# Output projection between the last rounds of a recurrence, and attention at the recurrence's priority, in a four-layer trunk

## The chip, the cores and the metric

One core of one Trainium2 chip runs the kernel. The metric is device time of one execution in microseconds, the median of several runs. The engines are TensorE (PE, with its weight loads as PEld), VectorE (DVE), ScalarE (ACT), GpSimd (POOL) and SyncE (SP), which here issues the DMA transfers. Each engine takes its own instructions in order.

## What is computed

A diffusion trunk of four layers over 256 latent and 256 context tokens (512 columns in all) with 1024 channels. Every layer is a pair of token mixers side by side, an output projection with a gated residual, and a SwiGLU channel mixer:

```
for l in range(DEPTH):                      # 4
    h_ = modulate(rmsnorm(h, norm_mix[l]), shift, scale)
    if l % 2 == 0:  y = concat(rwkv7_mixer(h_ @ ...), na_mixer(h_ @ ...))   # 512 + 512 channels
    else:           y = concat(gdn_mixer(h_ @ ...), s5_mixer(h_ @ ...))
    h = h + gate * (y @ w_out[l])
    h = h + gate2 * swiglu(modulate(rmsnorm(h, norm_ffn[l]), shift2, scale2))
```

`shift`, `scale` and `gate` come from an adaLN product with the conditioning vector (`mod_w`, 25 MB per layer). The RWKV-7 mixer is a recurrence over the tokens in both directions with 8 heads of 64 channels:

```
sa = einsum('bhvk,bhk->bhv', s, a_t)
s = s * w_t[:, :, None, :] + sa[..., None] * b_t[:, :, None, :] + v_t[..., None] * k_t[:, :, None, :]
y = einsum('bhvk,bhk->bhv', s, r_t)
```

It ends in a readout: group norm over each head, a bonus term and a gate. The attention is a softmax over a window of the grid for latent tokens and over the context, 8 heads of 64 channels. The change concerns layers 0 and 2, the even ones.

## The kernel before

**Layout.** Activations lie channel-major: the residual `hT` is [128 channels, 8 tiles, 512 tokens]. Large products split weights and activations into a high and a low part and take three matmuls per channel tile (`gemm`, lines 222 to 224: high by high, low by high, high by low), in groups of 256 output columns. Weights come by DMA from DRAM into `w` (line 187), a cast on ACT makes `wh` (line 190) and a subtraction on DVE makes `wl` (line 191). PSUM has eight banks by use: g, h, x and o one each, f and b two each; when `n.wide` is set, large products alternate between b, b and g, h, otherwise between g and h alone.

**Mixer of an even layer.** `even_layer` (line 1849) has eight units of the recurrence, four pairs of heads by two directions. `Pipe.run(i)` (line 1827), for i from 0 to 9, runs `front` of unit i, and by turns `mid` of unit i-1 and `rec` of unit i-2 (`together`, line 1812: one round is one turn of each). `rec` is the chain over the chunks of tokens: a state product on PE (line 784), an update of the state on DVE (line 793), copies on ACT (line 789) and a readout product (line 790). A pair's readout follows its second direction: DVE, ACT and POOL (lines 802 to 833) with two gate matmuls on PE (line 832). All of `Pipe.run` stands under `high_priority(PRIO)`. Attention (`Na.heads`, line 980) follows `run(3)` to `run(6)`, one pair of heads each, without priority: scores (line 1007), maximum, exponential and division (lines 1014 to 1018), transposes (line 1021) and the product with V (line 1033). `pump` (in `trunk`) puts adaLN products (line 165) between. The tile scheduler orders the instructions of each engine by priority, program order and a simulated time.

**Behind the mixer.** Each mixer's output tile goes to DRAM (`Mixed.put`, line 54), RWKV tiles 0 to 3 and attention tiles 4 to 7. When all is done, `split_y` (line 341) loads them back as `ev` and splits each into `nh` and `nl`, a cast on ACT (line 270) and a subtraction on DVE (line 271). `restore_h` loads the residual from DRAM, and `out_proj` runs 4 column groups x 8 channel tiles x 6 matmuls = 192 matmuls of 128x512, whose results `add_h` (line 335) adds to `hT` in halves. Then come the norm (square sums at line 284) and the channel mixer.

```
yh, yl, loaded = n.split_y(yt, tok)
...
n.wide = True
n.out_proj(l, yh, yl, tok)
```

In the stretches below, unit k of the recurrence begins with its first line 790 matmul.

Of the kernel before, what the change touches and what calls it, by code (L numbers as in the profile page):

```python
# [42 lines left out]
class Mixed:  # L43
    """Outputs of the mixers, channel-major, kept in DRAM by channel tile."""

    def __init__(self, n, ntok):
        self.n, self.ntok = n, ntok
        self.d = [n.dram.tile([128, NT], F32, name=f"yd{k}") for k in range(KT)]
# [4 lines left out]
    def put(self, k, y):  # L53
        self.n.nc.sync.dma_start(self.d[k][:, :self.ntok], y[:, :self.ntok])


class Net:
    def __init__(self, tc, a, ctx):
# [6 lines left out]
        # banks of PSUM by use: large products, parts of the mixers, adaLN, outputs of the mixers  # L65
# [13 lines left out]

    def load_consts(self, name, pool, tag=None, width=None):  # L80
# [22 lines left out]
    def restore_h(self, pool, tok):  # L103
        self.hT = pool.tile([128, KT, NT], F32, name="hT")
        for k in range(0, KT, 2):
            self.nc.sync.dma_start(self.hT[:, k:k + 2, tok], self.hd[:, k:k + 2, tok])

    def load_h(self, pool):
        nc = self.nc
        self.hT = pool.tile([128, KT, NT], F32, name="hT")  # L110
# [69 lines left out]
    def unit(self, src, kt, cols):  # L180
        """src [128, kt, cols] in DRAM -> high and low tiles."""
# [12 lines left out]
    def mm3(self, out, pairs, start=True, stop=True):  # L194
        """out += sum over (lhsH, lhsL, rhsH, rhsL) of lhs.T @ rhs."""
# [7 lines left out]
    def gemm(self, W, kt, c0, cols, xh, xl, tok, done, order=None):  # L203
        """Columns c0.. of W (given as [128, kt, n]), channel-major: done(column tile, psum) for each 128."""
        nc = self.nc
        nt = tok.stop - tok.start
        for u0 in range(c0, c0 + cols, 256):
# [7 lines left out]
            for i0 in range(0, kt, ku):  # L215
                kn, k0 = min(ku, kt - i0), ks[i0]
                wh, wl = self.unit(W[:, k0:k0 + kn, u0:u0 + n], kn, n)
                for kk in range(kn):
                    i, k = i0 + kk, k0 + kk
                    for (m, mm), p in zip(ms, ps):  # L220
# [3 lines left out]
                        nc.tensor.matmul(o, wl[:, kk, m:m + mm], xh[:, k, tok], start=False, stop=i == kt - 1)  # L224
            for (m, mm), p in zip(ms, ps):
                done((u0 - c0 + m) // 128, p[:mm, :nt])

    def gemm_tok(self, W, c0, cols, xh, xl, done):
        """Columns of W, token-major: done(token tile, first column, width, psum)."""
# [21 lines left out]
    def vecs(self, pool, name, **src):  # L251
        """Vectors of multiples of 128 in DRAM, channel-major [128, n] each; they become attributes of the result."""
# [20 lines left out]
    def square_sums(self, tok):  # L273
        """Sums of h^2 over the channels, token-major: [128, token tile]."""
# [13 lines left out]
    def rstd_bcast(self, tok, ss=None):  # L288
        """1 / sqrt(mean of h^2 + eps) on all partitions: [128, tokens]."""
# [16 lines left out]
    def norm_mod(self, l, g, which, tok, ss=None):  # L306
        """nH, nL: high and low parts of the modulated RMSNorm, channel-major."""
# [31 lines left out]
    ORDER = (4, 5, 6, 7, 0, 1, 2, 3)  # L339

    def split_y(self, y, tok):
        yh = self.gp.tile([128, KT, NT], F32R, name="nh")
        yl = self.gp.tile([128, KT, NT], F32R, name="nl")
        for k in self.ORDER:
# [3 lines left out]
        return yh, yl, last.ins  # L348

    def out_proj(self, l, yh, yl, tok):  # L350
        W = self.a["w_out"][l].rearrange("(j p) n -> p j n", p=128)
        self.gemm(W, KT, 0, D, yh, yl, tok, lambda k, p: self.add_h(l, 16, k, p, tok), self.ORDER)
# [79 lines left out]
def rows(x):  # L432
    """The four rows of the grid in a padded line of tokens."""
# [3 lines left out]
def rwkv_consts():  # L437
# [4 lines left out]
    # for a and for r, by the chunk of a tile: the mask of b on the chunk's half of the partitions, that of k on the other  # L442
# [14 lines left out]
class Rwkv:  # L457
    """Both directions of the time mixing for one layer, by pairs of heads."""
# [3 lines left out]
    def __init__(self, net, e, pool):  # L462
        self.n, self.nc, self.p, self.e = net, net.nc, pool, e
        self.a = net.a
# [15 lines left out]
        self.shb = pool.tile([128, 3, PADDED], F32, name="shb")  # L480
# [10 lines left out]
    def project(self, key, i, col, nh, nl):  # L491
        """Column tile col of the input projection as tile i of a group."""
# [13 lines left out]
    def shifted(self, key, cols):  # L506
        """A group of projections, mixed with the shift of the tokens."""
        nc, n, sh, pd = self.nc, len(cols), self.shb, self.pd[key]
        rk = self.p.tile([128, 2, NT], F32, name="rk", bufs=2)
        p = [rk[:, 0], rk[:, 1]]  # L510
        if n == 3:
            p.append(self.p.tile([128, NT], F32, name="v"))
# [9 lines left out]
        for i, c in enumerate(cols):  # L522
# [7 lines left out]
            else:  # L530
                # the two chunks of each tile in each other's place
# [8 lines left out]
    def lora_in(self):  # L540
        nc = self.nc
        x = self.shifted("L", [12, 13])
        self.tw = self.p.tile([128, NT], F32, name="tw")
# [1508 lines left out]
```

## Time and profile before

| | |
|---|---|
| runs, us | 3426.96, 3420.39, 3414.71; median 3420.39 |
| profiled execution: span, first to last instruction | 3398.9 us, 21.5 below that median |
| profiled execution's own time | only its span is given |
| PE, DVE, ACT, POOL busy | 92%, 56%, 38%, 15% of the span |
| mean granted TensorE clock | 0.929 of full speed |
| DMA | 479 MB, 141 GB/s over the span |

A windows row gives a stretch, its length, then the busy time and number of instructions of each engine in it, the granted TensorE clock, the share of time that the DMA engines were busy, and GB/s. A row of groups gives line, engine, operation, output<-inputs, shapes and count, then total busy us, mean ns of one, and idle time before them with what ended it. A timeline row gives start, length, engine, line, operation; in brackets the idle time before it and what released it.

### The profile page before, as it was taken

To read this page: it belongs to the slowest core of one execution; us is meant where nothing else is said; L and a number is where in the kernel's file an instruction comes from. 1 tells how busy PE (TensorE), PEld (TensorE's weight loads), DVE (VectorE), ACT (ScalarE), POOL (GpSimd) and SP (SyncE) were. 2 spreads that over 40 slices of the span, in tenths; PEclk is the share of its full clock that TensorE was granted. 3 is DMA by queue.
4 is the path that set the end of the run, shared out by engine and by line. 5 is a ranking of instruction groups with operands and counts; after the bars stand their busy time and mean duration, and the time that the engine had idled before them with its cause. 6 is when DMAs were issued, how large, how long until landed. Compare 5 with 4: busy or idle time off the path is not lost. (4 is left out here: it accounts for less than half of the span.)

```text
span 3398.9 us, 63286 instructions
## 1 busy us (share of the span) xinstructions
PE 3120.2 (92%) x24452; PEld 2418.1 (71%) x24452; DVE 1920.1 (56%) x4229; ACT 1291.6 (38%) x2785; POOL 515.4 (15%) x1159
## 2 busy tenths in 40 slices
PE   7999789999999889899999998877999999977998
PEld 4876456787787667578887776545787777756997
DVE  3556545766436696343434556555676445685554
ACT  3334344332235335232223333434333224534444
POOL 0223310000001653000000123220000000563000
PEclk8998889999999899899998998889999999978999
DMA  8635655345345544733336634553334334644554
GB/s 282 178 97 130 151 141 156 87 136 143 111 125 143 167 126 144 245 119 94 96 100 191 184 103 128 126 125 101 102 127 136 111 113 145 196 156 156 160 176 134
DMA packets 549696, 479.21 MB, mean 141 GB/s; under 512 B 176533, under 2 KB 480531, under 8 KB 549395
## 3 DMA queue, kind: packets, MB, share of 16 engines
q1 hardware_dynamic: 549394, 475.17, 48.5%
q8 instruction: 193, 3.16, 0.4%
q14 instruction: 109, 0.89, 0.1%
HBM read 406.34 MB, written 72.90 MB: 141 GB/s over the span
## 5 line engine op out<-in xcount | busy, mean ns | idle before, releaser
L191 DVE TENSOR_TENSOR wl<-w,wh 128x512 fp32r<-128x512 f32 x786 | 545.8, 697 | 766.4 <-ACT wh L190 746.6
L190 ACT CAST wh<-w 128x512 fp32r<-128x512 f32 x786 | 484.5, 619 | 1159.7 <-PE pb L223 343.3
L222 PE MATMUL pg<-nh,wh 128*128 128x512 f32 (+2 forms) x760 | 294.6, 388 | 19.4 <-ACT nh L270 8.7
L222 PE MATMUL pb<-nh,wh 128*128 128x512 f32 (+1 forms) x832 | 305.3, 374 | 4.0 <-ACT nh L325 2.7
L223 PE MATMUL pb<-nl,wh 128*128 128x512 f32 (+1 forms) x832 | 306.5, 371 | 0.0
L224 PE MATMUL pb<-nh,wl 128*128 128x512 f32 (+1 forms) x832 | 299.8, 373 | 0.0
L223 PE MATMUL pg<-nl,wh 128*128 128x512 f32 (+2 forms) x760 | 291.4, 383 | 0.6 <-DVE gr L1179 0.6
L224 PE MATMUL pg<-nh,wl 128*128 128x512 f32 (+2 forms) x760 | 290.4, 382 | 0.1
L298 POOL TENSOR_TENSOR nr<-nv,cst_base 128x4 f32<-128x4 f32 (+1 forms) x9 | 8.4, 938 | 1660.8 <-DVE nv L296 1660.8
L222 PE MATMUL ph<-nh,wh 128*128 128x512 f32 (+1 forms) x624 | 242.0, 388 | 10.1 <-ACT nh L325 5.9
L224 PE MATMUL ph<-nh,wl 128*128 128x512 f32 (+1 forms) x624 | 240.1, 385 | 0.0
L223 PE MATMUL ph<-nl,wh 128*128 128x512 f32 (+1 forms) x624 | 239.5, 384 | 0.0
L165 PE MATMUL px<-mw,cnd 128*32 128x256 f32 x1536 | 158.8, 450 | 83.5 <-DMA mw<-in_mod_w_dram 68.9
L222 PEld LDWEIGHTS pg<-nh,wh 128*128 128x128 f32 (+1 forms) x760 | 146.3, 193 | 56.4 <-ACT nh L270 11.3
L222 PEld LDWEIGHTS pb<-nh,wh 128*128 128x128 f32 x832 | 158.6, 192 | 36.3 <-ACT nh L325 3.2
L223 PEld LDWEIGHTS pb<-nl,wh 128*128 128x128 f32 x832 | 159.5, 192 | 29.3 <-DVE nl L271 1.3
L224 PEld LDWEIGHTS pb<-nh,wl 128*128 128x128 f32 x832 | 155.5, 191 | 30.7 <-issue 1.0
L223 PEld LDWEIGHTS pg<-nl,wh 128*128 128x128 f32 (+1 forms) x760 | 146.1, 192 | 34.8 <-issue 3.0
L224 PEld LDWEIGHTS pg<-nh,wl 128*128 128x128 f32 (+1 forms) x760 | 145.7, 192 | 29.1 <-issue 1.0
L858 POOL TENSOR_TENSOR Etmp<-E 64x14 f32<-64x14 f32 (+13 forms) x448 | 160.6, 359 | 31.1
L860 POOL TENSOR_TENSOR E<-E,Etmp 64x14 f32<-64x14 f32 (+13 forms) x448 | 158.8, 354 | 32.9
L222 PEld LDWEIGHTS ph<-nh,wh 128*128 128x128 f32 x624 | 119.6, 192 | 39.7 <-ACT nh L325 6.7
(578 smaller groups left out, 6440.8 us busy)
## 6 DMA issues: line engine op xcount, KB each, us to landing
mw<-in_mod_w_dram SPq DMA_DIRECT2D x192, 512.0 KB
w<-in_f_gate_dram SPq DMA_DIRECT2D x176, 256.0 KB
w<-in_f_up_dram SPq DMA_DIRECT2D x176, 256.0 KB
w<-in_f_down_dram SPq DMA_DIRECT2D x176, 256.0 KB
w<-in_w_in_even_dram SPq DMA_DIRECT2D x104, 256.0 KB
w<-in_w_in_odd_dram SPq DMA_DIRECT2D x80, 256.0 KB
w<-in_w_out_dram SPq DMA_DIRECT2D x64, 256.0 KB
hd<-hT SPq DMA_DIRECT2D x32, 256.0 KB
```

The source lines that it names most:

```text
L165: nc.tensor.matmul(p[32 * c:32 * c + 32, :256], self.cnd[:, k, :], wt[:, 256 * c:256 * c + 256], start=k == 0, stop=k == KT - 1, skip_grou ...
L190: nc.scalar.copy(wh[:, :n], w[:, :n])
L191: nc.vector.tensor_tensor(wl[:, :n], w[:, :n], wh[:, :n].bitcast(F32), op=ALU.subtract)
L222: nc.tensor.matmul(o, wh[:, kk, m:m + mm], xh[:, k, tok], start=i == 0, stop=False)
L223: nc.tensor.matmul(o, wh[:, kk, m:m + mm], xl[:, k, tok], start=False, stop=False)
L224: nc.tensor.matmul(o, wl[:, kk, m:m + mm], xh[:, k, tok], start=False, stop=i == kt - 1)
L298: nc.gpsimd.tensor_tensor(r, v, self.mhalf[:, :nt], op=ALU.pow)
L858: nc.gpsimd.tensor_tensor(o, E[:, :s, s:s + 1].to_broadcast([m8, s, v]), E[:, s:s + 1, s + 1:].to_broadcast([m8, s, v]), op=ALU.mult)
L860: nc.gpsimd.tensor_tensor(E[:, :s, s + 1:], E[:, :s, s + 1:], o, op=ALU.add)
```

## The change

Three things move in the even layers.

- `out_proj` is made in two parts. `EARLY`, channel tiles 0, 1 and 4 to 7, is loaded, split and multiplied while `run(8)` and `run(9)` go on; `LATE`, tiles 2 and 3 of the last two pairs of heads, follows the mixer. `gemm` becomes a generator, `gemm_steps`, that yields after each channel tile (six matmuls); after each round of `together` the pipe takes two steps in `run(8)` and one in `run(9)`, at ordinary priority and behind the last PE instruction put so far. The early part has only banks g and h. Its sum is added to `hT`, and that of the late part again.
- The last two pairs' outputs are split straight into `nh` and `nl` (`Mixed.put` with `parts` set), with no way through DRAM.
- `na.heads` stands under `high_priority(PRIO)`, as the recurrence does.

So that room is there by then, `hT` has a pool of its own, and the recurrence's tiles that only `front` needs lie in a pool `evenf` that is closed after `run(7)`, as attention's pool is. In odd layers `out_first` with all tiles stands for `split_y` and `restore_h` as before.

```diff
     def put(self, k, y):
-        self.n.nc.sync.dma_start(self.d[k][:, :self.ntok], y[:, :self.ntok])
+        if self.parts:
+            yh, yl = (x[:, k, :self.ntok] for x in self.parts)
+            self.n.split(y[:, :self.ntok], yh, yl)
+        else:
+            self.n.nc.sync.dma_start(self.d[k][:, :self.ntok], y[:, :self.ntok])
...
+    def last_pe(self):
+
+        return next(i for i in reversed(self.nc.cur_bb.bb.instructions) if i.engine == mybir.EngineType.PE)
...
+                    if i < kt - 1:
+                        yield
             for (m, mm), p in zip(ms, ps):
                 done((u0 - c0 + m) // 128, p[:mm, :nt])
+            yield
...
-    def split_y(self, y, tok):
+    EARLY, LATE, ALL = (0, 1, 4, 5, 6, 7), (2, 3), (4, 5, 6, 7, 0, 1, 2, 3)
+
+    def out_first(self, l, y, tok, ks):
+
+        self.open_g(3)
+        self.open_h()
         yh = self.gp.tile([128, KT, NT], F32R, name="nh")
         yl = self.gp.tile([128, KT, NT], F32R, name="nl")
-        for k in self.ORDER:
+        for k in ks:
             t = self.gp.tile([128, PADDED], F32, name="ev", bufs=2)[:, :NT]
             last = self.nc.sync.dma_start(t[:, tok], y.d[k][:, tok])
             self.split(t[:, tok], yh[:, k, tok], yl[:, k, tok])
-        return yh, yl, last.ins
-
-    def out_proj(self, l, yh, yl, tok):
+        y.parts = yh, yl
+        with self.tc.issue_after(last.ins):
+            self.restore_h(tok)
+        return last.ins, self.out_proj(l, y, tok, ks)
...
+FILL = (2, 1)
...
         steps = [s for s in steps if next(s, steps) is not steps]
+        yield
...
-            together(*(getattr(self.m, f)(*u(i - k), self.S[u(i - k)[0]])
-                       for k, f in enumerate(self.m.parts, 1) if u(i - k)))
+            for r in together(*(getattr(self.m, f)(*u(i - k), self.S[u(i - k)[0]])
+                                for k, f in enumerate(self.m.parts, 1) if u(i - k))):
+                with self.n.tc.high_priority(-PRIO), self.n.tc.issue_after(self.n.last_pe()):
+                    for _ in range(FILL[i == len(self.units) + len(self.m.parts) - 1]):
+                        next(self.fill, None)
...
             for h in heads.get(i, ()):
-                na.heads(h, yt)
+                with n.tc.high_priority(PRIO):
+                    na.heads(h, yt)
             pump(3)
...
+            if i == 7:
+                first_.__exit__(None, None, None)
+                np_.__exit__(None, None, None)
+                loaded, pipe.fill = n.out_first(l, yt, tok, n.EARLY)
+        for _ in pipe.fill:
+            pass
+    return yt, loaded
...
             n.wide = True
-            n.out_proj(l, yh, yl, tok)
+            if l % 2:
+                loaded, proj = n.out_first(l, yt, tok, n.ALL)
+            else:
+                proj = n.out_proj(l, yt, tok, n.LATE)
+            for _ in proj:
+                pass
```

How many PE instructions of attention (lines 1007, 1021 and 1033) and of the output projection stand in each part of the program's order, before -> with the change:

| | unit 2 | unit 3 | unit 4 | unit 5 | unit 6 | unit 7 | last readout | behind it |
|---|---|---|---|---|---|---|---|---|
| layer 0, attention | 32 -> 45 | 38 -> 59 | 34 -> 47 | 34 -> 39 | 38 -> 16 | 16 -> 0 | 14 -> 0 | |
| layer 0, projection | | | | | 0 -> 24 | 0 -> 109 | 0 -> 17 | 192 -> 42 |
| layer 2, attention | 34 -> 64 | 34 -> 60 | 38 -> 50 | 32 -> 30 | 32 -> 0 | 16 -> 0 | 22 -> 0 | |
| layer 2, projection | | | | | 0 -> 94 | 0 -> 50 | 0 -> 6 | 192 -> 42 |

The order of PE in layer 2, inside the last unit's rounds, before (`st`, `Bst`, `Phi` are the state and its factors, `naP` the softmax, `naqk` queries and keys):

```order
L784 MATMUL pb<-Bst,Phi 64x64 x2
L1021 MATMUL pg<-cst_base,naP 128x128 x2
L784 MATMUL pb<-st,Phi 64x64 x2
L790 MATMUL po<-st_17575,RW 64x128
L784 MATMUL pb<-st,Phi 64x64 x2
L1007 MATMUL ph<-naqk,naqh 128x512
L1007 MATMUL ph<-naqk 128x512
L784 MATMUL pb<-st,Phi 64x64 x2
L790 MATMUL po<-st_17576,RW 64x128
L790 MATMUL po<-st_17573,RW 64x128
```

and with the change (lines 784, 790, 222 to 224 are now 815, 821, 237 to 239):

```order
L815 MATMUL pb<-Bst,Phi 64x64 x2
L237 MATMUL pg<-nh,wh 128x512
L238 MATMUL pg<-nl,wh 128x512
L239 MATMUL pg<-nh,wl 128x512
L237 MATMUL ph<-nh,wh 128x512
L238 MATMUL ph<-nl,wh 128x512
L239 MATMUL ph<-nh,wl 128x512
L815 MATMUL pb<-st,Phi 64x64 x2
L821 MATMUL po<-st_17612,RW 64x128
```

Scores and transposes of the attention are gone from the round, and one step of the projection, six matmuls, stands between two state products.

The order of DVE in layer 0, in the last unit's rounds, before:

```order
L793 SCALAR_TENSOR_TENSOR st<-pb,Dk,Bst 128x64
L1014 TENSOR_REDUCE mx<-pg 128x1
L793 SCALAR_TENSOR_TENSOR st<-pb,Dk,Bst 128x64 x2
L1017 RECIPROCAL sm<-sm 128x1
L1018 TENSOR_SCALAR naP<-naP,sm 128x512
L793 SCALAR_TENSOR_TENSOR st<-pb,Dk,Bst 128x64
L1014 TENSOR_REDUCE mx<-pg 128x1
```

and with the change (793 is now 824, 335 is 357, 191 is 206):

```order
L824 SCALAR_TENSOR_TENSOR st<-pb,Dk,Bst 128x64
L357 SCALAR_TENSOR_TENSOR hT<-ph,mod,hT 128x256 x2
L357 SCALAR_TENSOR_TENSOR hT<-pg,mod,hT 128x256 x2
L824 SCALAR_TENSOR_TENSOR st<-pb,Dk,Bst 128x64
L206 TENSOR_TENSOR wl<-w,wh 128x512 x2
L824 SCALAR_TENSOR_TENSOR st<-pb,Dk,Bst 128x64
L206 TENSOR_TENSOR wl<-w,wh 128x512
L357 SCALAR_TENSOR_TENSOR hT<-ph,mod,hT 128x256 x2
```

Between two state updates DVE had the softmax's maximum and division; it now has additions into the residual and subtractions that make the weights' low part.

## Rows read from the trace of the kernel before

**Rows 1.** The page: the span, and busy time of the engines.

```profile
span 3398.9 us, 63286 instructions
...
PE 3120.2 (92%) x24452; PEld 2418.1 (71%) x24452; DVE 1920.1 (56%) x4229; ACT 1291.6 (38%) x2785; POOL 515.4 (15%) x1159
```

**Rows 2.** Windows of layer 0: upstream, last rounds, tail, behind the mixer.

```profile
core 0: us, PE busy (x) PEld busy (x) DVE busy (x) ACT busy (x) POOL busy (x), PEclk, DMA share, GB/s
315.00:512.00 197.00, 159.07 (x2244) 101.58 (x2227) 111.70 (x289) 81.18 (x219) 53.62 (x130) 0.82 0.60 145
512.00:548.30 36.30, 34.59 (x437) 21.39 (x436) 20.30 (x56) 21.51 (x66) 0.00 (x0) 0.95 0.39 122
548.30:560.00 11.70, 7.00 (x38) 3.88 (x38) 8.21 (x16) 5.57 (x12) 2.07 (x1) 0.86 0.29 93
560.00:612.00 52.00, 51.39 (x237) 41.49 (x237) 23.87 (x68) 15.68 (x27) 0.00 (x0) 0.97 0.61 169
```

**Rows 3.** Windows of layer 2, the same four stretches, the same columns.

```profile
2108.60:2306.00 197.40, 160.26 (x2182) 102.67 (x2181) 113.27 (x287) 79.78 (x215) 52.65 (x128) 0.82 0.51 120
2306.00:2347.60 41.60, 32.78 (x401) 21.33 (x401) 20.70 (x58) 21.12 (x66) 4.60 (x4) 0.88 0.17 52
2347.60:2357.20 9.60, 7.13 (x45) 3.99 (x44) 6.02 (x14) 3.92 (x10) 2.07 (x1) 1.00 0.01 2
2357.20:2410.00 52.80, 46.32 (x210) 36.91 (x209) 25.71 (x71) 18.04 (x31) 0.00 (x0) 0.97 0.65 182
```

**Rows 4.** Timeline of PE, layer 2: last readout matmul, first of the output projection.

```profile
2356.62 0.59 PE L832 MATMUL pb<-sx,g 128*128 128x512 f32 x1
2362.27 0.76 PE L222 MATMUL pg<-nh,wh 128*128 128x512 f32 x1 [5.06 <-ACT nh L270]
```

**Rows 5.** Windows of PE, late stretches: lines 1007, 1021 and 1033, each both layers.

```profile
512.00:560.00 48.00, 5.18 (x16) 0.93 0.37 115
2306.00:2357.20 51.20, 5.78 (x18) 0.90 0.14 42
...
512.00:560.00 48.00, 5.37 (x28) 0.93 0.37 115
2306.00:2357.20 51.20, 5.39 (x28) 0.90 0.14 42
...
512.00:560.00 48.00, 8.31 (x48) 0.93 0.37 115
2306.00:2357.20 51.20, 8.48 (x48) 0.90 0.14 42
```

**Rows 6.** Timeline of PE, layer 0: output projection at its own pace.

```profile
573.03 0.39 PE L224 MATMUL ph<-nh,wl 128*128 128x512 f32 x1
...
581.43 0.39 PE L224 MATMUL ph<-nh,wl 128*128 128x512 f32 x1
```

**Rows 7.** Groups by line, DVE then ACT, over the whole span.

```profile
L335 DVE SCALAR_TENSOR_TENSOR hT<-pb,mod,hT 128x256 f32<-128x256 f32 x140 | 58.6, 477 | 33.3 <-PE pb L224 33.3
...
L1018 DVE TENSOR_SCALAR naP<-naP,sm 128x512 f32<-128x512 f32 (+1 forms) x64 | 27.1, 423 | 1.6
...
L271 DVE TENSOR_TENSOR nl<-ev,nh 128x512 fp32r<-128x512 f32 (+1 forms) x32 | 19.6, 625 | 32.8 <-ACT nh L270 32.5
...
L1014 DVE TENSOR_REDUCE mx<-pg 128x1 f32<-128x512 f32 (+1 forms) x32 | 17.7, 553 | 4.6 <-PE pg L1007 4.1
...
L1016 ACT ACTIVATE naP<-ph,mx 128x512 f32<-128x512 f32 (+1 forms) x32 | 18.6, 580 | 22.6 <-DVE mx L1014 22.0
...
L270 ACT CAST nh<-ev 128x512 fp32r<-128x512 f32 (+1 forms) x32 | 18.1, 567 | 41.9 <-DMA ev<-yd 41.6
```

**Rows 8.** Timeline of layer 2, unit 7: two state updates that follow each other.

```profile
2341.06 0.28 DVE L793 SCALAR_TENSOR_TENSOR st<-pb,Dk,Bst 128x64 f32<-128x64 f32 x1
...
2341.85 0.27 DVE L793 SCALAR_TENSOR_TENSOR st<-pb,Dk,Bst 128x64 f32<-128x64 f32 x1
```

**Rows 9.** Waits of PE, layer 0, upstream and last rounds: total, times, longest.

```profile
PE px L165 <- DMA mw<-in_mod_w_dram: 26.1, 15, 5.5
PE pg L1007 <- ACT naP L1016: 4.6, 3, 3.5
```

More of the change, by code (lines that the diff above doesn't have):

```diff
@@ L78, in close_g, with open_h, close_h @@
         self.gp = None
+    def open_h(self):
+        self.hc_ = self.tc.tile_pool(name="h", bufs=1, side="right")
+        self.hT = self.hc_.__enter__().tile([128, KT, NT], F32, name="hT")
+    def close_h(self):
+        self.hc_.__exit__(None, None, None)
+    def last_pe(self):
+        return next(i for i in reversed(self.nc.cur_bb.bb.instructions) if i.engine == mybir.EngineType.PE)
     def load_consts(self, name, pool, tag=None, width=None):
@@ L101, in save_h, with restore_h @@
         self.hd = hd
-    def restore_h(self, pool, tok):
-        self.hT = pool.tile([128, KT, NT], F32, name="hT")
+    def restore_h(self, tok):
         for k in range(0, KT, 2):
@@ L460, with __init__ @@
     parts = ("mid", "rec")
-    def __init__(self, net, e, pool):
+    def __init__(self, net, e, pool, first):
         self.n, self.nc, self.p, self.e = net, net.nc, pool, e
+        self.pf = first
         self.a = net.a
@@ L479, in __init__ @@
         self.W = a["w_in_even"][e].rearrange("(j p) n -> p j n", p=128)
-        self.shb = pool.tile([128, 3, PADDED], F32, name="shb")
+        self.shb = first.tile([128, 3, PADDED], F32, name="shb")
         self.sts = [pool.tile([128, 128], F32, name=f"st{i}") for i in range(4)]
@@ L542, in lora_in @@
         x = self.shifted("L", [12, 13])
-        self.tw = self.p.tile([128, NT], F32, name="tw")
+        self.tw = self.pf.tile([128, NT], F32, name="tw")
         nc.scalar.activation(self.tw[0:64], x[0][0:64], AF.Tanh)
@@ L582, in pre @@
         r, k, v = self.shifted(hp, [hp, 4 + hp, 8 + hp])
-        lora = pl.tile([128, 2, 128], F32, name="lora", bufs=2)
+        lora = self.pf.tile([128, 2, 128], F32, name="lora", bufs=2)
         g2 = pl.tile([128, 128], F32, name="g2", bufs=2)
@@ L610, in front @@
         nc, n, pl = self.nc, self.n, self.p
-        t1 = lambda name: pl.tile([128, NT], F32, name=name)
+        t1 = lambda name: self.pf.tile([128, NT], F32, name=name)
         ch = lambda x: x.rearrange("p (c t) -> p c t", t=64)
@@ L643, in front @@
         ar, X["r"] = self.ar[:, 0:k4 + 1:k4], self.ar[:, k4]
-        bk = pl.tile([128, 8, 2, 64], F32, name="bk")
+        bk = self.pf.tile([128, 8, 2, 64], F32, name="bk")
         bq = bk.rearrange("p (t c) b s -> p t (c b) s", c=2)
@@ L1825, in __init__ @@
         self.S, self.late = {}, None
+        self.fill = iter(())
     def run(self, i):
@@ L1997, in trunk @@
             n.save_h()
+            n.close_h()
             fp.__exit__(None, None, None)
-            yt = odd_layer(n, l, nh, nl, pump, weights) if l % 2 else even_layer(n, l, nh, nl, pump)
-            n.open_g(3)
-            yh, yl, loaded = n.split_y(yt, tok)
+            layer = odd_layer if l % 2 else even_layer
+            yt, loaded = layer(n, l, nh, nl, pump, tok, *((weights,) if l % 2 else ()))
             fp = tc.tile_pool(name=f"f{l + 1}", bufs=1)
             f = fp.__enter__()
-            with tc.issue_after(loaded):
-                n.restore_h(f, tok)
             n.wide = True
-            n.out_proj(l, yh, yl, tok)
+            if l % 2:
[3 more added lines that the diff above has]
+            for _ in proj:
+                pass
             pump(8)
@@ L2025, in trunk @@
         fp.__exit__(None, None, None)
+        n.close_h()
         n.close_g()
```

28 lines of the change are left out of this document (15 added, 13 removed).

## The prediction, made before the change was run

> **What bounds the kernel now.** I read the page first: TensorE (PE) is busy 3120.2 of 3398.9 us [rows 1], so only work that PE does not repeat, and PE's idle time, can move the end. Then I cut layers 0 and 2 into stretches by the recurrence's own instructions and read each engine's busy time in them [rows 2, 3]. Four stretches matter per layer: *upstream* (units 2 to 5 of the recurrence, whose rounds also carry the next units' front and mid), the *last rounds* (units 6 and 7), the *tail* (last readout, from the last state product to the last L832), and what follows the mixer. In layer 0 they last 197.00, 36.30, 11.70 and 52.00 us with PE busy 159.07, 34.59, 7.00 and 51.39; in layer 2 197.40, 41.60, 9.60 and 52.80 with 160.26, 32.78, 7.13 and 46.32. So PE has 37.9 and 37.1 us idle upstream, 1.7 and 8.8 us in the last rounds, 4.7 and 2.5 us in the tails. Behind the mixer PE is full but for one hole in layer 2: 5.06 us before its first output-projection matmul, which waits for a cast of a tile that has just been to DRAM and back [rows 4].
>
> The last rounds are not empty. They carry attention: 18.86 us of PE in the late stretches of layer 0 (5.18 + 5.37 + 8.31) and 19.65 us in layer 2 (5.78 + 5.39 + 8.48) [rows 5]. To put 150 projection matmuls there, the change must first send that attention upstream. The question is what it costs there.
>
> **The change, part by part.**
>
> *Projection leaves the end.* Of 192 matmuls per even layer, 150 stand ahead of the last L832 and 42 behind it. They take one every 0.2333 us (573.03 to 581.43 us holds 36) [rows 6], so 150 x 0.2333 = 35.0 us leave the stretch behind the mixer, in each layer. Tiles 2 and 3 are now split straight from the readout. Behind the last readout the projection waits for a cast and a subtraction (0.567 + 0.625 us) [rows 7] and a start, 1.5 us in all; the 5.06 us hole of layer 2 goes. Layer 0: -35.0 + 1.5 = -33.5. Layer 2: -35.0 + 1.5 - 5.06 = -38.5.
>
> *Last rounds.* Layer 0: 38 rows of attention leave them (54 of 68 late rows stood in rounds, 16 stay), at 18.86/68 = 0.277 us each 10.5 us; 133 projection matmuls enter, 31.0 us. PE 34.59 - 10.5 + 31.0 = 55.1 us. Layer 2: 48 rows at 19.65/70 = 0.281 leave, 13.5 us; 144 matmuls enter, 33.6 us: 32.78 - 13.5 + 33.6 = 52.9 us. Idle time that stays: at least 0, at most the 8.8 us of layer 2's own rounds; I take 2.5, near the 1.7 of layer 0's, whose PE also had other work in the queue at every step. The state's own steps come every 0.8 us with nothing between (2341.06 to 2341.85) [rows 8], below the 1.4 us of the six matmuls put between them, so PE and not the state chain sets these rounds. Layer 0: 57.6 for 36.30, **+21.3**. Layer 2: 55.4 for 41.60, **+13.8**.
>
> *Tails.* Attention leaves (14 and 22 rows), 17 and 6 projection matmuls enter: about PE's 7 us again or less, beside a chain of DVE, ACT and POOL that sets the length. 0.
>
> *Attention upstream.* 52 rows (14.4 us) in layer 0 and 70 (19.65 us) in layer 2 move into stretches with 37.9 and 37.1 us of idle PE. Lowest: 0, all of it falls into holes; a gain is excluded, since none of its work goes (a rise of the clock is a rival below). The longest wait there is for adaLN weights still in transfer, 26.1 us in 15 waits [rows 9], which other work can fill. Highest as PE work: all of it, 34.1 us. With equal priority the program's order decides, and attention then stands ahead of the next unit's chain, not behind it: not only holes are filled. I take half: +7.2 and +9.8.
>
> *Second accumulation.* Two passes over the channels mean 16 more additions into the residual per layer, 32 x 0.477 = 15.3 us of DVE [rows 7]. With subtractions and weight splits DVE stays near 35 of some 55 us in the last rounds, so 0; cover gone, this is a rival below. The casts, subtractions, 12 weight loads, 6 reloads of mixer tiles and 4 of the residual per layer are moved, not added (four stores and four reloads even go), and pass SP's queue earlier, in stretches whose DMA share is 0.39 and 0.17: 0. Two odd layers: the same instructions, 0.
>
> Layer 0: -33.5 + 21.3 + 7.2 = -5.0. Layer 2: -38.5 + 13.8 + 9.8 = -14.9. **Sum -19.9 us.** It is made against the profiled execution; its span is 21.5 us below the median of the runs (3420.4), and I let that distance stand: **3400 us**. Bounds of the terms: idle in the rounds 0 to 8.8 (-5 to +12.6 in both layers), attention 0 to all (-17 to +17).
>
> **The rivals.**
>
> *A: the clock rises in fuller rounds.* The granted clock is 0.82 upstream in both layers, 0.95 and 0.88 in the last rounds, 0.97 behind them [rows 2, 3]. Busy time above full clock is about 0.18 x 159.07 + 0.05 x 34.59 + 0.18 x 160.26 + 0.12 x 32.78 = 63 us. If denser rounds win half of it back, the time falls by a further 31.5 us: 3400 - 32 = 3368. For it: the densest stretches (51.39 of 52.00 busy) have the highest clock. Against it: layer 0's stretch at 0.82 is 81% busy, as layer 2's, and it is 128-wide transposes and small products that are added upstream. The Trainium skill ("TensorE: Matmul & The Clock Gate", Loop structure matters more than you think) holds that matmuls kept back to back stay at the high clock, which by itself would give this time; the rows agree for the projection, 0.97. The same page (Part 4: PE-mode transpose) says that transposes do not count as busy in the same way, which would leave the upstream clock where it is.
>
> *B: attention stands in the recurrence's way: slower.* Engines take instructions in order. What moves upstream (122 rows, 6.5 per query tile, 18.8 tiles) is 34.1 us of PE, 18.8 x (0.553 + 0.423) = 18.3 us of DVE and 18.8 x 0.580 = 10.9 us of ACT [rows 7], and a row of one engine waits for another: a scores product that waits for the softmax of the tile before (4.6 us in three waits already) [rows 9] now blocks the chain behind it. If all PE work and half of the 29.2 us of DVE and ACT come on the path, 48.7 us stand in place of my 17.0: 3400 + 32 = 3432. It turns the sign from 37 us upstream on, and 47 us would be measured as slower. For it: equal priority and program order. Against it: 75 us of idle PE and DVE at 57% upstream.
>
> *C: the projection stalls in the last rounds.* The early pass has two PSUM banks, g and h, where the wide pass behind the mixer alternates with two more; all four column groups must be drained by four additions of 0.477 us before the next may start: 1.9 us x 8 = 15.3 us. If the reloads are late as in layer 2 before, add 5.06 per layer: 25.4 us, 3425, no difference to be measured. For it: additions queue on an in-order DVE behind state updates. Against it: a blocked PE also has adaLN products and the state's products to do, if they stand ahead of the blocked row.
>
> That the change doesn't do what it says is excluded by the order: 150 of 192 matmuls do stand ahead of the last readout, in both layers.
>
> **How the numbers follow.** A difference under 0.3% (10 us) can't be told from none here: faster is below 3410, slower above 3431. Forecast 0.47, its own range 3386 to 3412 from the bounds above (both ends together are unlikely); A 0.16, B 0.19, C 0.18. Faster: the forecast's part below 3410 (0.43) and A, 0.59. B and C lie about the upper bound: of B 0.12 and of C 0.07 end above 3431, slower 0.19. Same is what is left, 0.04 + 0.07 + 0.11 = 0.22. To leave 2 in 10 out, the range reaches to A and to B: 3362 to 3434.
>
> **What would show it.** Right: in the changed profile some 42 projection matmuls behind the last L863 per layer, 10 to 12 us from there to the first square sums' work instead of some 45; last rounds of 55 to 60 us with PE idle under 4; upstream stretches of 204 and 207 us. A would show as an upstream clock above 0.86. B as upstream stretches above 215 us, with PE waiting for naP or for the state. C as PE waiting in the last rounds for L357's additions or for hT and ev. The forecast is wrong if the upstream stretches don't lengthen at all, or if the last rounds grow by more than the matmuls put into them.

## The result, and the profile of the changed kernel

The changed kernel takes 3457.8 us (median of 4 runs, 3455.0 to 3465.0) against 3423.6 for the kernel before: a ratio of **1.0102, interval 1.0078 to 1.0127**. It is slower by 1.0%, and outside the predicted range.

The page of the changed kernel, answering to [rows 1]:

```profile
span 3457.7 us, 63374 instructions
...
PE 3164.3 (92%) x24452; PEld 2440.6 (71%) x24452; DVE 1933.9 (56%) x4261; ACT 1289.6 (37%) x2785; POOL 516.2 (15%) x1159
```

The profile of before that the prediction was made from has a span of 3398.9 us, some 20 us under the runs that were timed. A second profile of the same kernel (the run `again` below) has 3412.7, and stretches are compared with that one. Windows of it, first the five stretches of layer 0, then of layer 2 (from the norm to unit 1, units 2 to 5, last rounds, tail, behind the mixer; columns as in [rows 2]):

```profile
22.30:314.50 292.20, 268.79 (x2607) 201.72 (x2607) 156.55 (x354) 108.46 (x240) 60.06 (x165) 0.93 0.60 167
314.50:514.10 199.60, 165.79 (x2214) 106.06 (x2206) 110.47 (x288) 81.24 (x219) 50.90 (x130) 0.79 0.60 143
514.10:550.50 36.40, 34.88 (x438) 21.50 (x436) 20.32 (x56) 21.54 (x66) 0.00 (x0) 0.94 0.39 119
550.50:562.20 11.70, 7.00 (x37) 3.92 (x38) 8.33 (x16) 5.56 (x12) 2.07 (x1) 0.88 0.27 88
562.20:620.80 58.60, 55.69 (x261) 44.48 (x260) 26.16 (x74) 17.50 (x30) 1.01 (x1) 0.97 0.57 160
...
1841.90:2114.60 272.70, 260.93 (x2472) 198.40 (x2471) 149.97 (x341) 106.52 (x235) 57.92 (x164) 0.93 0.57 155
2114.60:2310.30 195.70, 160.50 (x2181) 102.33 (x2179) 114.51 (x288) 79.83 (x215) 52.66 (x127) 0.81 0.52 121
2310.30:2352.70 42.40, 33.85 (x402) 21.88 (x402) 20.70 (x58) 21.17 (x66) 4.61 (x4) 0.84 0.17 52
2352.70:2362.30 9.60, 7.11 (x44) 3.96 (x44) 6.02 (x14) 3.89 (x10) 2.07 (x1) 1.00 0.01 2
2362.30:2426.60 64.30, 56.12 (x261) 44.93 (x261) 29.30 (x78) 20.36 (x36) 1.01 (x1) 0.95 0.57 162
```

The same ten stretches of the changed kernel:

```profile
22.90:333.00 310.10, 273.76 (x2622) 205.63 (x2620) 160.23 (x364) 107.45 (x240) 61.28 (x170) 0.90 0.56 156
333.00:538.20 205.20, 176.29 (x2239) 112.00 (x2237) 118.73 (x307) 91.98 (x247) 52.72 (x125) 0.83 0.57 140
538.20:599.30 61.10, 60.33 (x554) 41.65 (x550) 26.45 (x59) 24.36 (x64) 0.00 (x0) 1.00 0.56 187
599.30:611.60 12.30, 8.56 (x28) 5.54 (x29) 7.82 (x16) 2.25 (x4) 2.07 (x1) 0.79 0.21 64
611.60:634.00 22.40, 19.56 (x111) 16.68 (x110) 14.27 (x56) 7.94 (x13) 1.01 (x1) 0.88 0.43 76
...
1873.50:2155.80 282.30, 262.04 (x2542) 196.48 (x2541) 156.35 (x351) 107.47 (x238) 59.86 (x161) 0.94 0.55 147
2155.80:2380.30 224.50, 192.11 (x2279) 122.39 (x2278) 124.54 (x325) 95.24 (x254) 50.09 (x129) 0.76 0.52 126
2380.30:2435.90 55.60, 55.50 (x419) 39.58 (x419) 23.72 (x53) 20.12 (x53) 0.00 (x0) 0.96 0.32 101
2435.90:2447.20 11.30, 5.73 (x17) 3.52 (x18) 6.20 (x12) 1.45 (x3) 2.14 (x1) 0.80 0.09 23
2447.20:2469.00 21.80, 19.46 (x112) 16.45 (x110) 14.29 (x56) 7.95 (x14) 1.01 (x1) 0.89 0.45 78
```

Read as differences, what was meant to happen did: the end is shorter by 36.2 and 42.5 us, the last rounds longer by 24.7 and 13.2, with PE busy for all but 0.8 and 0.1 us of them. The losses stand elsewhere. Units 2 to 5, which took the attention, are longer by 5.6 and 28.8 us; from the norm to unit 1, where nothing was to change, 17.9 and 9.6 are lost. Layer 0 comes out 12.6 us longer, layer 2 10.8. And layer 1, whose code the change hardly touches, is 17.8 us longer, layer 3 1.8. That is 43.0 of the 45.0 us between the two spans. The medians of the timed runs are only 34.2 us apart, so some 11 us of these differences are scatter of single profiles. The DMA hole of layer 2 [rows 4] is gone; the timeline of PE in the changed kernel:

```profile
2445.14 2.08 PE L863 MATMUL pb<-sx,g 128*128 128x512 f32 x2
2446.22 1.42 PE L237 MATMUL pb<-nh,wh 128*128 128x512 f32 x1
2447.44 0.63 PE L238 MATMUL pb<-nl,wh 128*128 128x512 f32 x1
2447.86 0.63 PE L239 MATMUL pb<-nh,wl 128*128 128x512 f32 x1
2448.29 0.63 PE L237 MATMUL pb<-nh,wh 128*128 128x512 f32 x1
```

### The profile page after: what moved, and what is told of

Same layout as the page of the kernel before. It is cut to its first block, busy times and chain, and to the rows that moved or that the text cites. A ratio compares the mean times of both kernels' runs of the same rounds, so it can differ in the third digit from the quotient of the medians.

```text
span 3457.7 us, 63374 instructions
## 1 busy us (share of the span) xinstructions
PE 3164.3 (92%) x24452; PEld 2440.6 (71%) x24452; DVE 1933.9 (56%) x4261; ACT 1289.6 (37%) x2785; POOL 516.2 (15%) x1159
## 5 line engine op out<-in xcount | busy, mean ns | idle before, releaser
L237 PE MATMUL pg<-nh,wh 128*128 128x512 f32 (+1 forms) x784 | 306.7, 391 | 9.6 <-ACT nh L347 3.3
L239 PE MATMUL pg<-nh,wl 128*128 128x512 f32 (+1 forms) x784 | 301.4, 384 | 2.1 <-DVE wl L206 2.1
L238 PE MATMUL pg<-nl,wh 128*128 128x512 f32 (+1 forms) x784 | 301.7, 385 | 1.5 <-DVE nl L293 1.0
L237 PE MATMUL ph<-nh,wh 128*128 128x512 f32 (+2 forms) x648 | 253.6, 391 | 12.4 <-ACT nh L347 6.1
L238 PE MATMUL ph<-nl,wh 128*128 128x512 f32 (+2 forms) x648 | 251.2, 388 | 0.7 <-DVE nl L348 0.7
L239 PE MATMUL ph<-nh,wl 128*128 128x512 f32 (+2 forms) x648 | 251.2, 388 | 0.3 <-DVE wl L206 0.3
L237 PEld LDWEIGHTS pg<-nh,wh 128*128 128x128 f32 x784 | 151.8, 194 | 49.2 <-issue 6.9
L238 PEld LDWEIGHTS pg<-nl,wh 128*128 128x128 f32 x784 | 151.6, 193 | 36.2 <-issue 3.2
L239 PEld LDWEIGHTS pg<-nh,wl 128*128 128x128 f32 x784 | 151.3, 193 | 35.1 <-DVE wl L206 3.0
L237 PEld LDWEIGHTS pb<-nh,wh 128*128 128x128 f32 x784 | 149.2, 192 | 34.2 <-ACT nh L347 3.4
L237 PEld LDWEIGHTS ph<-nh,wh 128*128 128x128 f32 (+1 forms) x648 | 125.2, 193 | 44.1 <-ACT nh L347 7.3
```

What stands on the lines that cost most here:

```text
L237: nc.tensor.matmul(o, wh[:, kk, m:m + mm], xh[:, k, tok], start=i == 0, stop=False)
L238: nc.tensor.matmul(o, wh[:, kk, m:m + mm], xl[:, k, tok], start=False, stop=False)
```

## The experiments

Three theories were put to the test. *Theory 1*: attention at the recurrence's priority costs more upstream than the end gains (the prediction's rival B). *Theory 2*: the two passes of the projection cost. *Theory 3*: the scheduler, which orders every engine by a simulated time, deals a new order in all four layers as soon as anything is edited, and the loss is that of the new deal.

### The parts of the change

**The kernel before again** (no edit):

> The kernel before, unchanged, for a second profile: is its first one (span 3398.9 us, 21 to 25 below the median of its runs) a fair base for a comparison by stretches? If so the mixers of layers 1 and 3 (end of the norm's broadcast to the next one) again last 422.0 and 351.0 us, and units 1 to 5 of layers 0 and 2 together 508 us (254.7 and 253.3). If that profile was a lucky one, the 20 us lie somewhere here, and what looked like a loss in the odd layers (+20.6 and +9.9 us in the changed kernel) shrinks by as much.

3414.6 us, span 3412.7, layers 1 and 3 at 424.8 and 359.1 us. So the first profile was 8 us lucky in layer 3, and what looked like a loss of 9.9 us there is 1.8. The loss in layer 1 stays.

**Without the attention's priority**:

```diff
-                with n.tc.high_priority(PRIO):
-                    na.heads(h, yt)
+                na.heads(h, yt)
```

> The change without the attention's priority. The order leaves 82 and 70 attention matmuls in or behind unit 6, and only 24 and 26 projection matmuls get ahead of the last readout. Theory 1 (attention at the recurrence's priority is what costs, in units 1 to 5): units 1 to 5 return to the lengths of before within 8 us per layer, and the whole to 3415 to 3435 us. Theory 2 (the two passes of the projection, its two banks and its 32 more additions cost): still some 20 us above before, 3440 to 3455. Theory 3 (the odd layers, dealt anew, cost 30 us whatever is done to the even ones): layer 1, whose order is near that of before, is back at 422, layer 3, whose order is near that of the change, stays at 360; total 3435 to 3445.

3479.5 us, 1.0186 (1.0164 to 1.0207): the worst but one, above all three expectations. Windows of its two tails:

```profile
576.90:608.90 32.00, 21.40 (x79) 13.26 (x80) 16.27 (x34) 13.03 (x28) 2.15 (x1) 0.73 0.29 90
...
2404.00:2428.20 24.20, 16.13 (x72) 10.78 (x72) 12.87 (x25) 10.64 (x22) 2.15 (x1) 0.79 0.44 134
```

Attention is now still running when the early pass is issued, both end up in the tail of the chain, and the tails take 32.0 and 24.2 us instead of 11.7 and 9.6. As dealt here, the early pass needs the priority. With so few projection matmuls ahead, the run can't tell what the priority itself costs.

**The attention's priority alone** (that edit, in the kernel before):

> The kernel before with the attention's priority alone; the projection stays behind the mixer (42 matmuls of layer 2 slip ahead by themselves), and no attention is left from unit 6 (layer 0) or 7 (layer 2) on. Theory 1: units 1 to 5 are 20 to 35 us longer per layer than before, the last rounds shorter by the attention that has left them (10 to 14 us per layer); total 3450 to 3475 us. Theory 2: no second pass, so no loss: 3410 to 3430. Theory 3: the even layers within 5 us of before, the odd ones longer by 10 to 30.

3443.7 us, 1.0075 (1.0054 to 1.0097). Up to unit 5 layer 0 loses 24 us, layer 2 only 10; layer 2 as a whole is 11 us *faster* than before (573.7 for 584.6), with 42 matmuls of its projection ahead by themselves, and layer 1 is 16 us slower (441.1) with not a line of it changed. No theory had all of that. Theory 2 is not needed for a loss: there is no second pass here.

**The projection held behind the mixer**:

```diff
-FILL = (2, 1)
+FILL = (0, 0)
...
-        for _ in pipe.fill:
-            pass
+        with n.tc.issue_after(n.last_pe()):
+            for _ in pipe.fill:
+                pass
```

> The change with every matmul of the output projection held behind the mixer, so that attention goes upstream and nothing takes its place in the last rounds. Theory 1: units 1 to 5 as long as in the changed kernel (+24 and +36 us, less where its order differs), last rounds 24 to 30 us instead of 61 and 56, 192 matmuls (45 us) behind the mixer instead of 42; total above the changed kernel by 0 to 15 us, 3458 to 3475. Theory 2: two passes without interleaving; near 3430. Theory 3: its layer 1 has an order of its own (half like that of the change), so it need not be 442; a value near 422 would say that the loss there hangs on the deal.

3458.6 us, 1.0127 (1.0102 to 1.0151), at the lower end of what Theory 1 expected and far from Theory 2's 3430. Layer 1 is at 438.0. Its window of the last rounds of layer 0, now without attention and without projection:

```profile
530.60:568.50 37.90, 32.05 (x420) 20.05 (x416) 15.32 (x37) 17.83 (x53) 0.00 (x0) 0.83 0.71 236
```

They last 37.9 us, where they lasted 36.4 with attention in them: in that order the attention had cost nothing there. (In the five other orders of the kernel before, below, these rounds take 43.7 to 47.6 us.) In layer 2 they shrink, 42.4 to 34.6. From here to the changed kernel the early pass adds 23.2 and 21.0 us to the rounds for 133 and 144 matmuls (31 and 34 us of work) and takes 38 and 39 off the end: between a quarter and two fifths of the pass's work is hidden, as far as two kernels with an order each can say.

### An empty edit, and the change by layer

**An empty edit of the kernel before**:

```diff
-                na.heads(h, yt)
+                with n.tc.high_priority(0):
+                    na.heads(h, yt)
```

> The kernel before with an empty edit: attention stands under a priority of 0, the same instructions, the same priority, but the scheduler deals another order (12, 40, 28, 40, 34 and 20 attention matmuls in units 2 to 7 of layer 0 for 32, 38, 34, 34, 38 and 16, 32 in and behind the last readout for 14; half of a quarter of the order of layer 1 changes too). Theory 3, widened after the first four runs (each edit makes the scheduler deal anew, and most of the loss is the new deal, not the moved work): 3435 to 3470 us, layer 1's mixer near the 435 us that the run without the attention's priority showed with the same order, layer 0's above 605. Theory 1 (the attention's priority costs): no priority, no loss: 3411 to 3427 us and layers 0 and 1 within 5 us of before.

3454.4 us, **1.0105** (1.0065 to 1.0144). The computation is the same, and each engine has as many instructions of work as before; their order alone differs, and the loss is that of the whole change. (The edit is not quite empty for the scheduler: `high_priority` sets the running count of priorities back when it is left, so what follows the attention ranks level with it.) Layer 0 takes 616.9 us and layer 1 438.6, as Theory 3 expected. Its page:

```profile
span 3436.0 us, 63333 instructions
...
PE 3126.1 (91%) x24452; PEld 2409.8 (70%) x24452; DVE 1919.6 (56%) x4229; ACT 1293.3 (38%) x2785; POOL 518.2 (15%) x1159
```

Span less busy time is PE's idle time: 309.9 us, where the second profile of before has 276.7. So an order alone can lose as much as the whole change. What the moved work costs in the changed kernel is not yet shown by that.

**The priority in layer 2 alone**, in the kernel before:

```diff
-                na.heads(h, yt)
+                if l == 2:
+                    with n.tc.high_priority(PRIO):
+                        na.heads(h, yt)
+                else:
+                    na.heads(h, yt)
```

> The kernel before with the attention's priority in layer 2 alone; the order of layers 0 and 1 is that of before, instruction for instruction. Theory 3: layers 0 and 1 within 4 us of before (598 and 424); layer 2 as its deal falls, near the 574 us of the run with the priority in both layers, whose layer 2 has much the same placing: total 3405 to 3420. Theory 1: layer 2's units 1 to 5 are 15 to 35 us longer, total 3430 to 3455.

3421.2 us, 1.0016 (0.9992 to 1.0039): no difference, against Theory 1 and 1 us above Theory 3's range. Layer 2 takes 579.7 us, 5 under before, again with 42 projection matmuls ahead; layer 1 stays at 426.9, and layer 0 is 6 us longer (604.8) for the 4 expected.

**The whole change in layer 0 alone** (the attention's priority under the same condition):

```diff
-            if i == 7:
+            if i == 7 and l == 0:
...
-            if l % 2:
+            if l % 2 or not (l == 0):
                 loaded, proj = n.out_first(l, yt, tok, n.ALL)
```

> The whole change in layer 0 alone; layers 0 and 1 have the order of the changed kernel, instruction for instruction, layer 2 attention late and the projection behind the mixer as before. Theory 3: layer 1 again at 440 to 445 us though nothing of its code differs from before, layer 0 at 608 to 614; total 3440 to 3470 depending on the deal of layer 2. Theory 1: layer 0 +13 us, the rest as before: 3425 to 3440.

3487.3 us, 1.0193 (1.0151 to 1.0234), above what was expected: layer 2, dealt anew, takes 615.5 us. Layer 1 in the two runs with the old order and in the two with the new one, windows of the whole mixer (the kernel before again, then priority in layer 2, then the changed kernel, then the change in layer 0):

```profile
1022.30:1447.10 424.80, 380.57 (x3299) 287.78 (x3298) 272.21 (x557) 179.67 (x398) 144.27 (x277) 0.90 0.54 163
```
```profile
1030.10:1457.00 426.90, 380.01 (x3299) 287.54 (x3298) 271.64 (x557) 180.08 (x398) 143.61 (x277) 0.91 0.53 162
```
```profile
1037.70:1480.30 442.60, 387.50 (x3299) 292.25 (x3298) 273.19 (x557) 178.78 (x398) 148.24 (x277) 0.88 0.51 155
```
```profile
1046.30:1485.40 439.10, 386.46 (x3299) 291.26 (x3298) 273.41 (x557) 178.90 (x398) 148.24 (x277) 0.89 0.51 156
```

The same 3299 PE instructions: 425 and 427 us in one order, 443 and 439 in the other.

**The whole change in layer 2 alone** (`l == 2` in those conditions; in the other layers `hT` and the tiles of `front` stay in the pools of before):

```diff
-        self.open_h()
+        if l == 2:
+            self.open_h()
```

> The whole change in layer 2 alone, with layer 0 in the order of before, instruction for instruction, and layer 1 nearly so (96 in 100). Only 93 projection matmuls get ahead of the end of the last readout. Theory 3: layers 0 and 1 within 5 us of before, so the loss of the whole change shrinks to layer 2's own: 0 to 12 us; total 3415 to 3435, faster than before only if layer 2's deal is a good one. Theory 1: units 1 to 5 of layer 2 carry the whole loss (+38 us there) against the 42 us that leave the end and the 13 that the last rounds grow: total 3425 to 3445.

3417.2 us, 0.9996 (0.9973 to 1.0020). Layer 2 takes 573.7 us, 11 less than before. Layer 1 took 440.0 in this profile, although 96 of 100 of its PE rows stand as before. The profiles above of one and the same order lie 2 to 4 us apart in that layer; whether the few moved rows or the scatter of a profile made the 15 us here is not shown.

### Pairs with the same empty edit

If the deal moves the time by 1%, the moved work can only be read over several deals. So both kernels were given the same edits that change no computation (called empty here): a priority of 0 around the first `pump(3)` of a step (p2) or around the second (p6), and `SAVE`, the amount by which the residual's store is put back, at 40 (p4) or 0 (s0) for 60.

```diff
-            pump(3)
+            with n.tc.high_priority(0):
+                pump(3)
```
```diff
-SAVE = 60
+SAVE = 0
```

> The kernel before, dealt anew by an empty edit (the first adaLN pump of each step under a priority of 0): 84, 56, 91 and 72 of 100 PE rows of the mixers of layers 0 to 3 keep their place. Theory 3 (a new deal alone costs): 3435 to 3470 us, as the first empty edit. Theory 1 (the moved work costs): 3411 to 3430.

> The changed kernel with the same empty edit; still 150 projection matmuls ahead of the last readout's end in both layers. Theory 3: 3425 to 3465, on either side of the same edit of the kernel before, the difference of the pair between -25 and +20 us. Theory 1: 25 to 50 us above the pair's other half.

> The kernel before, dealt anew by another edit that moves no mixer work (the priority of the residual's store, SAVE, 40 for 60): 80, 80, 76 and 91 of 100 PE rows of the mixers keep their place. Theory 3: 3430 to 3465 us. Theory 1: 3411 to 3430.

> The changed kernel with SAVE at 40; 129 and 150 projection matmuls ahead of the last readout's end. Theory 3: 3425 to 3465, within 25 us of the pair's other half on either side; with the pair before and the unedited pair the mean difference is then below +20 us. Theory 1: 25 to 50 us above the pair's other half.

> The kernel before, dealt anew by an empty edit (the second adaLN pump of each step under a priority of 0). Theory 3 (a new deal alone costs): 3440 to 3470 us, 0.6 to 1.5 per cent above before, with PE's idle time 300 to 325 us where the profiles of before have 273 to 275. Theory 1 (the moved work costs): 3411 to 3430.

> The changed kernel with that empty edit. Theory 3: 3425 to 3465, PE's idle time 275 to 295 us, below its partner's by some 25, given back as busy time (matmuls of the projection between others, and a lower clock in units 1 to 5 of layer 2). Theory 1: 25 to 50 us above its partner.

> The kernel before, dealt anew by SAVE at 0 for 60 (the priority of the residual's store). Theory 3: 3440 to 3470 us. Theory 1: 3411 to 3430.

> The changed kernel with SAVE at 0; 93 and 150 projection matmuls ahead of the last readout's end. Theory 3: 3425 to 3465, within 25 us of its partner on either side. Theory 1: 25 to 50 us above its partner.

| edit | kernel before, us and ratio | PE idle | changed kernel, us and ratio | PE idle |
|---|---|---|---|---|
| none | 3423.6, 1 | 276.7 | 3457.8, 1.0102 | 293.4 |
| attention at 0 | 3454.4, 1.0105 | 309.9 | | |
| p2 | 3454.4, 1.0103 | 316.6 | 3456.6, 1.0127 | 292.5 |
| p4 | 3463.0, 1.0131 | 324.5 | 3434.9, 1.0061 | 279.7 |
| p6 | 3447.2, 1.0072 | 296.4 | 3437.4, 1.0056 | 296.5 |
| s0 | 3465.8, 1.0137 | 310.2 | 3399.0, 0.9951 | 258.3 |
| SAVE 20 (below) | | | 3429.1, 1.0022 | 280.6 |

All ratios are to the unedited kernel before, with intervals of 0.002 to 0.005 to each side; idle is span less PE busy of one profile. Every one of five empty edits makes the kernel before slower, most of all p4 and s0, which shift the rank of the residual's stores alone. In the four pairs the changed half is higher once (p2), lower three times, and never the 25 to 50 us above its partner that Theory 1 expected. Theory 3's ranges hold for seven of the eight times. s0 of the changed kernel lies 26 us below its range and 67 below its partner, p4 is 28 us below its partner for the 25 allowed, and the idle time of p6 does not differ in its pair (296.4 and 296.5) where some 25 us less were expected. (For the kernel before that expectation has 273 to 275 us of idle time; its two profiles have 278.7 and 276.7.)

Two more runs: the best one again, apart from its choice, and one more deal (`SAVE` at 20).

> The changed kernel with SAVE at 0, the same kernel as in the run a_s0, measured anew. If its gain is its order's: again 0.992 to 0.999 of the kernel before, 3390 to 3415 us, with layer 2's mixer near 570 us and layer 1's near 427. If it was chance of the measurement: 1.000 to 1.006.

> The changed kernel with SAVE at 20, one more deal: 93 and 129 projection matmuls ahead of the last readout's end. Theory 3 (the deal decides): anything from 3395 to 3465 us, so far 0.995 to 1.013 of before. If the moved work gains by itself some 20 us over an average deal of the old order (1.011): most likely 3420 to 3450.

The first is 3400.3 us, **0.9936** (0.9908 to 0.9964), against 0.9951 the first time: the gain is its order's, and this kernel, the change with `SAVE = 0`, beats both. The second is 1.0022 (1.0001 to 1.0043). The page of the first:

```profile
span 3398.3 us, 63328 instructions
...
PE 3134.9 (92%) x24452; PEld 2431.9 (72%) x24452; DVE 1935.8 (57%) x4261; ACT 1291.1 (38%) x2785; POOL 510.6 (15%) x1159
```

Over the deals, the old order edited has a mean ratio of 1.0110 (5 deals, 1.0072 to 1.0137), the changed kernel 1.0053 (6 deals, 0.9951 to 1.0127): a difference of -0.0057 with a standard error of 0.0028 from these spreads, some -20 us. That is two standard errors: it leans to a gain from the moved work, and does not settle it. It also leaves the unedited kernel before out of one mean and keeps the unedited changed kernel in the other. With it as a sixth deal the difference is -0.0038, little over one standard error (0.0033). What is shown is that an order alone loses as much as the one changed kernel, and that over the deals the moved work makes no loss that can be seen.

The deals of the changed kernel differ in more than luck: they do not move the same amount of work. The two that put all 300 projection matmuls of both layers ahead are the two slowest (none and p2: 1.0102, 1.0127), those with 279 lie between (p4 and p6: 1.0061, 1.0056), and those with 243 and 222 are the fastest (s0 and SAVE 20: 0.9951, 1.0022). The upstream stretches go the same way. Over all orders in which the attention has its priority, units 2 to 5 take 218 to 227 us where at most 6 of a layer's 256 attention matmuls are left behind the start of unit 6 (5 stretches), and 197 to 217 us where 28 to 40 are left (14 stretches). Two of them, layer 2 of p2 and of s0, each a row of PE alone:

```profile
2149.40:2376.50 227.10, 193.98 (x2283) 0.76 0.52 126
2125.60:2323.40 197.80, 174.28 (x2233) 0.80 0.54 127
```

No run sets that number by itself, so this goes together and is not shown as a cause. It keeps Theory 1 open for the last part of the attention.

## Why the prediction was wrong

The step that failed is the sum's last one: "It is made against the profiled execution". The sum took every stretch that the change does not name to stand as it was, "Two odd layers: the same instructions, 0" above all. The instructions were the same; their order was not. Layer 1 alone shows it: 425 us in the order of before, 443 in that of the changed kernel. Of the 64.9 us between the forecast of -19.9 and this deal's +45.0, 47.1 stand in stretches that were put at 0 (17.9, 9.6, 17.8 and 1.8 in the table), and 17.4 in the attention upstream, nearly all of them in layer 2 (+28.8 for +9.8). Nor is the order of before an average one: the mean of its five empty edits is 1.1% slower. No rival held that. Neither of the prediction's two signs of being wrong appeared (the upstream stretches did lengthen, and the last rounds grew by less than the matmuls put into them), since both watch only stretches that the change names. The terms themselves, in us, layer 0 and layer 2, predicted; in this one changed kernel against the second profile of before; and as the difference of the means over the 6 and 5 deals above, one profile each:

| term | predicted | this deal | means over deals |
|---|---|---|---|
| end | -33.5, -38.5 | -36.2, -42.5 | -42.3, -42.3 |
| last rounds | +21.3, +13.8 | +24.7, +13.2 | +9.5, +18.7 |
| tail | 0, 0 | +0.6, +1.7 | +2.2, +1.3 |
| units 2 to 5 | +7.2, +9.8 | +5.6, +28.8 | +10.0, +10.1 |
| norm to unit 1 | 0, 0 | +17.9, +9.6 | +8.7, +3.7 |
| sum | -5.0, -14.9 | +12.6, +10.8 | -12.0, -8.4 |
| layers 1 and 3 | 0, 0 | +17.8, +1.8 | +0.6, +2.2 |
| whole | -19.9 | +45.0 | -16.3 |

(The deals of the last column move 93 to 150 projection matmuls per layer, the prediction 150. Single numbers spread: units 2 to 5 of layer 2 lie between 189 and 209 us in the old order, between 197 and 227 in the changed.)

- *Projection leaves the end*: right, and the hole of layer 2 went with it. The late pass takes more than its 42 x 0.2333 us, since it starts at the low one of the clock's two levels (1.2 and 2.4 GHz), behind a tail with 5.73 of 11.30 us busy. In the timeline above its matmuls stand 0.43 us apart where PE runs without a pause, and the granted clock is 0.50 there and 1.00 right after:

```profile
2446.20:2449.50 3.30, 3.30 (x8) 2.24 (x7) 0.93 (x7) 0.62 (x1) 0.00 (x0) 0.50 0.09 14
2451.70:2455.00 3.30, 3.30 (x14) 2.70 (x15) 3.20 (x13) 2.28 (x4) 0.00 (x0) 1.00 0.83 92
```

- *Last rounds*: right in this deal, within 3.4 us. PE does set them: 60.33 of 61.10 and 55.50 of 55.60 us busy.
- *Attention upstream*: half of it was a choice between two bounds. It came near on the mean and in layer 0, which is luck as much as reading. In layer 2 of this deal all of its 19.65 us came on the path and more. Units 2 and 3 carry it; windows of the first profile of before, then of the changed kernel:

```profile
2108.60:2163.00 54.40, 48.90 (x515) 32.16 (x513) 36.88 (x92) 22.42 (x58) 25.18 (x62) 0.74 0.44 92
2163.00:2214.00 51.00, 42.88 (x703) 27.87 (x702) 30.84 (x77) 20.71 (x57) 11.48 (x28) 0.87 0.49 133
```
```profile
2155.80:2228.50 72.70, 62.19 (x499) 38.41 (x498) 40.52 (x107) 29.09 (x74) 20.41 (x59) 0.72 0.47 94
2228.50:2304.40 75.90, 61.84 (x679) 38.64 (x678) 42.13 (x106) 29.86 (x79) 16.88 (x37) 0.65 0.53 122
```

  PE is 32.3 us busier in them, for 56 more rows of attention (some 16 us by the 0.281 of the prediction; 68 matmuls, since the table of placings counts the two heads of line 1033 as one) and 22 more matmuls of adaLN. The rest goes with the granted clock, 0.65 for 0.87 in the second unit. There 32 matmuls of one line and shape took 442 ns each for 288:

```profile
L674 PE MATMUL pf<-ar,bk 64*128 64x128 f32 x32 | 4.0, 288 | 0.0
L705 PE MATMUL pf<-ar,bk 64*128 64x128 f32 x32 | 6.6, 442 | 0.0
```

  Waiting adds to it. The waits of PE over units 0 to 5 of layer 2 show what rival B named (`naP`), 8.9 us of it, where B's sum has 14.6 for both layers:

```profile
PE px L180 <- DMA mw<-in_mod_w_dram: 15.0, 5, 5.2
PE ph L1038 <- ACT naP L1047: 8.9, 3, 8.2
```

- *Rival A* (the clock rises) holds only where the projection went: 0.94 and 0.84 became 1.00 and 0.96 in the last rounds. The mean clock of this deal fell, 0.925 to 0.917. By the Trainium skill ("TensorE: Matmul & The Clock Gate", Loop structure matters more than you think) dense matmuls keep the high clock; the rounds agree. Upstream, where the added work is small products and transposes, the clock of units 2 to 5 fell in layer 2 (0.81 to 0.76) and rose in layer 0 (0.79 to 0.83). Over the deals it does not fall: the means in layers 0 and 2 are 0.80 and 0.78 for the kernel before, 0.83 and 0.79 for the changed one.
- *Rival B* gave a time (3432) nearer to the measured one. Its sign came in layer 2 (224.5 us upstream, with waits for `naP`) and not in layer 0 (205.2), and it has no loss in layer 1. The priority alone (1.0075) is no worse than an empty edit, so no cost of its own can be shown; what the deals say of the last part of the attention leaves it open. *Rival C* did not happen in this deal: in the last rounds PE is idle for 0.8 and 0.1 us in all.
- Over the deals PE's idle time falls by 28 us (311.5 to 283.5, means of the table, without the unedited kernel before and its 276.7), which is what the change is for. 12 us come back as busy time (3138 to 3150).

Open is why some orders of layer 1 take 425 to 427 us and others 434 to 450. Its busy time differs by 7 us and its idle time by 11 between the windows above; no single wait accounts for it. That the residual has a pool of its own in the changed kernel does not explain it: the first empty edit, with the pools of before, has 438.6.

## What to carry to other kernels

Where a scheduler deals the order from a simulated time, an edit anywhere re-deals what follows, and its measured effect is its own work plus the difference of two deals. Before such a change is judged at 1%, give both kernels a few edits that change no computation (a priority of 0, another rank for one store), compare the means, look at what else the deals differ in, and keep the best one: here the deals of one kernel lie 1.4 to 1.8% apart, and the best of the changed one is 0.6% below the kernel before. And work that is put into a stretch with other filler only gains what the filler does not lose where it goes: count the filler that has to leave, and try moving less of it: here the even layers of the changed kernel whose order left about a seventh of the attention behind took less time (layer 2: 570 to 583 us) than those that moved nearly all of it (593 to 596).

## What the runs showed of the hardware that was not expected

The same 3299 matrix instructions of a mixer took 425 and 427 us in one order, 443 and 439 in another. The runs of the unchanged kernel on the chips used here lie between 3403 and 3439 us, so that a single profile per kernel cannot place a difference of 10 us. And in the changed kernel the granted clock was as low as 0.65 over a unit in which attention stood between the recurrence's products (0.87 over the same unit of before, with less of it), and 0.96 to 1.00 over rounds that the projection filled.
